# Decode products of a RetNet/HGRN2 step in plain float32 on the four column quarters of TensorE, with W_out loaded a second time

## The chip, the cores and the metric

The kernel runs on one core of a Trainium2 chip. The metric is the device time of one launch in microseconds (us). Three runs of the kernel before gave 1083.44, 1084.49 and 1085.34 us, so the median is 1084.49 us.

In what follows PE is TensorE's matmul, PEld its weight load, DVE is VectorE, ACT is ScalarE, POOL is GpSimd and SP is SyncE, which here only issues DMAs. A line such as L557 is a line of the kernel before; where the changed kernel is meant, the text says so.

## The reference

One layer is computed for a new prompt of 2048 tokens and for 8 sample tokens ("decode" below). Both share the weights. All data is float32.

```python
h = rmsnorm(x, norm_g)
rq, rk, rv, rg, hq, hf, hi, hgate = split(h @ w_in, 8)        # each 512 wide
# 4 retention heads of 128: rotary q and k, fixed decay per head
o_ret, s_ret_new = chunked_decay_recurrence(rq, rk, rv, log_gamma, s_ret)
# 4 HGRN2 heads of 128: silu(hq), gate f = lb + (1-lb) sigmoid(hf), k = 1-f
o_hg, s_hg_new = chunked_decay_recurrence(silu(hq), kin, hi, logf, s_hg)
# S_t = diag(f_t) S_{t-1} + k_t v_t^T ;  o_t = S_t^T q_t
o = concat(head_rmsnorm(o_ret) * silu(rg), head_rmsnorm(o_hg) * silu(hgate))
y = rmsnorm(x + o @ w_out, final_norm_g)
```

For the prompt the state starts at zero and the recurrence is done in chunks of 128 tokens. Each of the 8 decode tokens has a state of its own for each of the 8 heads (128x128), so that a head has one step `S = f*S + k v^T`, `o = S^T q` for each token. The new states of prompt and decode are outputs too.

## The kernel before

**Arithmetic.** Most matmuls run in fp32r with a split: an operand is written as a high and a low part (`hi_lo`, L106 on ACT and L107 on DVE), and a product is three matmuls (high·high, high·low, low·high; `three`, L292, and the projections, L557). The small score, state and transposition matmuls are plain float32.

**Stages, by the time in the profile.** From 7 to about 175 us stands the *values stage* (`pv`, L292): the 512+512 value columns of the projection for 16 token blocks. The first four blocks (pairs 0 and 1) are plain products, `pv0` while the weights still arrive, `pv1` after that; later pairs use a Strassen-like scheme of seven products, whose weight sums (`T1` to `T4`) are made by `wv_comb` on DVE, and whose token sums by `tok_ops`. From about 175 to 895 us stands the *recurrence stage*: 16 units of some 45 us, each with the projections of one head for one half of the prompt (L557) and, between them, the recurrence of the unit before. HGRN2 heads have score matmuls of 32 columns, which stand on the four column quarters of the array (`pah`, `plh`; L813, L832). From 895 to 957 us comes the *output stage* for the first token blocks (`py`, L1203), and from 957 to 1071 us six *out pairs* of 19 us (`po`, L292; pairs 2 to 7), again seven products of 12 matmuls each with operands that DVE makes out of `o_dram` (the steps `op_a`, `op_s12`, `op_s34`, `op_s23`, `op_s14`, `op_a22` for the pair that follows).

**Decode.** Three decode products are made with 40-column weights (8 columns of high part, 24 of zeros, 8 of low part) and 512 moving columns, 32 matmuls each:
- `pvd` (L400, `decode_values`): the values of the 8 tokens, after the plain products of block pair 1, 16 matmuls for each kind of head; `xs_hl` holds the split tokens.
- `pd` (L981, `d_mm`): `S^T q` of one head for all 8 tokens, against the split state `dsh`, `dsl` (made by `d_lo`: L969 on ACT, L973 on DVE). All 8x8 products of token and state are made and only the diagonal is used. Each head goes through `d_load`, `d_mul`, `d_add`, `d_lo` and two `d_mm`, at positions between units 8 and 15.
- `pyd` (L1029, `d_project`): the output projection, at 937 us; ahead of it `d_norm`, `d_sq`, `d_ms`, `d_rs` normalise and `d_tr` transposes, head by head (`pdt`, L1018).

**What sets the order.** PE's order is written out by hand, by the steps in program order and their positions (`place`, `merge`, `side_at`). On the other engines a scheduler orders the instructions by priority as their operands come free; SP, ACT's and POOL's queues issue their DMAs in that order, one after another. A tile pool of six 4 KB buffers, `rawp` (tag `raw`), holds the raw weights of the recurrence stage (`wr`), the decode states `dS`, the values `dv`, the splits `ds`, and in the out pairs `or` and `oS`; a new tile waits until the readers of the one that had its buffer are done.

Of the kernel before, what the change touches and what calls it, by code (L numbers as in the profile page):

```python
# [41 lines left out]
def step_kernel(ctx, tc, a, out):  # L42
# [15 lines left out]
    d_dram = dr.tile([8, 42240], F32, tag="d_dram", name="d_dram")  # L58
# [319 lines left out]
    xs_hl = vq.tile([P, KT, 40], F32R, tag="xs_hl", name="xs_hl")  # L378

    def decode_inputs():  # L380
        msd = sm.tile([NB, 2], F32, tag="msd", name="msd")
        for h in range(2):
# [6 lines left out]
        dve.tensor_tensor(xs, xs, g_in.unsqueeze(2).to_broadcast([P, KT, NB]), op=ALU.mult)  # L389
        act.activation(xs_hl[:, :, 0:8], xs, AF.Copy)  # L390
        act.activation(xs_hl[:, :, 8:32], zero.unsqueeze(1).to_broadcast([P, KT, 24]), AF.Copy)
        dve.tensor_tensor(
            xs_hl[:, :, 32:40], xs, xs_hl[:, :, 0:8].bitcast(F32), op=ALU.subtract
        )

    def decode_values(ty):
        ps = bank([40, GW], f"pvd{ty}")
        for k in range(KT):
            for n, w in enumerate(wv(f"B{k // 4 + 1}{ty + 1}", k % 4)):
                pe.matmul(ps, xs_hl[:, k], w, start=(k == 0 and n == 0), stop=(k == KT - 1 and n == 1))  # L400
        t1 = vq.tile([NB, GW], F32, tag="vo", name=f"vd1{ty}", bufs=2)
        act.activation(t1, ps[32:40, :], AF.Copy)
        t2 = vq.tile([NB, GW], F32, tag="vo", name=f"vd2{ty}", bufs=2)
        dve.tensor_tensor(t2, ps[0:NB, :], t1, op=ALU.add)
        dve.tensor_scalar(t2, t2, rsd[:, ty : ty + 1], None, op0=ALU.mult)
        sp.dma_start(vd_dram[ty], t2)
# [35 lines left out]
    wv_load(5)  # L442
    for k in (1, 5):
        x_split0(0, k)
        wv_split(k)
# [13 lines left out]
    sp.dma_start(pk, a["pack"])  # L459
# [20 lines left out]
    for ty in (1, 0):  # L480
# [10 lines left out]
        decode_values(ty)  # L491
# [437 lines left out]
    def d_split(src, name):  # L929
        pl, tag = (up, "dhl") if name == "dq_hl" else (rawp, "raw")  # L930
        t = pl.tile([P, 8, 40], F32R, tag=tag, name=name)
        act.activation(t[:, :, 0:8], src, AF.Copy)
        act.activation(t[:, :, 8:32], zero.unsqueeze(1).to_broadcast([P, 8, 24]), AF.Copy)
        dve.tensor_tensor(t[:, :, 32:40], src, t[:, :, 0:8].bitcast(F32), op=ALU.subtract)
        return t

# [18 lines left out]
    def d_add(hd):  # L955
# [6 lines left out]
        if hd == 0:  # L962
            dec["q"] = d_split(dq, "dq_hl")

    def d_lo(hd):
        ty, h = divmod(hd, NH)
        S, vb = dec["l", hd]
        sh, sl = (rawp.tile([P, NB, P], F32R, tag="raw", name=f"ds{t}{hd}") for t in "hl")
# [4 lines left out]
        dve.tensor_tensor(sl, S, sh.bitcast(F32), op=ALU.subtract)  # L973
        dec["s", hd] = (sh, sl)

    def d_mm(hd, part):
        for i in (part,):
            e = tp.tile([40, 512], F32, tag="tmp", name=f"de{hd}{i}")
            pt = ps_o.tile([40, 512], F32, tag="o", name=f"pd{hd}{i}")
            for n, t in enumerate(dec["s", hd]):  # L980
                pe.matmul(  # L981
                    pt, dec["q"][:, hd], t[:, i * 4 : i * 4 + 4], start=(n == 0), stop=(n == 1)
                )
            act.activation(e, pt, AF.Copy)
            act.dma_start(
                d_dram[hd, : 40 * D].rearrange("(r c) -> r c", c=D)[:, i * 512 : i * 512 + 512], e
            )

    def d_norm():
        dec["o2"] = []  # L990
        for n in range(2):
            x = rawp.tile([NB, 8, P], F32, tag="raw", name=f"do{n}")
            o0 = n * 32 * D
            pool.dma_start(
                x, d_dram[:, o0 : o0 + 8 * 1152].rearrange("u (b c) -> b u c", c=1152)[:, :, :P]
            )
            dec["o2"].append(x)

    def d_sq():
        o, sq = dec["o2"]  # L1000
        dve.tensor_tensor(o, o, sq, op=ALU.add)
        dve.tensor_tensor(sq, o, o, op=ALU.mult)

    def d_ms():
        ms = sm.tile([NB, 8], F32, tag="dms", name="dms")
        dve.tensor_reduce(ms, dec["o2"][1], axis=mybir.AxisListType.X, op=ALU.add)
# [3 lines left out]
    def d_rs():  # L1010
        o = dec["o2"][0]
        dve.tensor_tensor(o, o, dec["ms"].unsqueeze(2).to_broadcast([NB, 8, P]), op=ALU.mult)
        dec["o"] = o

    def d_tr():
        pt = ps_tr.tile([P, 8, NB], F32, tag="tr", name="pdt")
        for hd in range(8):
            pe.transpose(pt[:, hd], dec["o"][:, hd], ident[:NB, :NB])  # L1018
        dve.tensor_tensor(dq, pt, dg_, op=ALU.mult)
# [458 lines left out]
```

## Time and profile before

| | |
|---|---|
| median of three runs | 1084.49 us |
| the profiled execution, its time and its span | 1081.12 us, 1079.3 us |
| mean granted TensorE clock | 0.998 |
| PE busy | 1061.1 us, 98% |
| DVE busy | 742.4 us, 69% |
| ACT busy | 407.3 us, 38% |
| POOL busy | 125.8 us, 12% |
| moved by DMA | 146.76 MB, mean 136 GB/s |

The profiled execution is one launch; its time is 3.4 us below the median of the three others. Busy time of PE counts from a matmul's start to its modelled end, so that 98% busy does not say that matmuls start as fast as they can. A plain float32 matmul leaves two records in the trace, an fp32r matmul one.

### The profile page before, as it was taken

Reading aid. Unit: us, or ns where it says so; the run is one execution under the profiler, and the core shown is the slowest. Engines: PE = TensorE matmul, PEld = TensorE weight load, DVE = VectorE, ACT = ScalarE, POOL = GpSimd, SP = SyncE. Lnnn points to the kernel's source line nnn. Section 1 sums busy time; section 2 is a strip of 40 time slices with the busy share of each in tenths; the row PEclk is TensorE's granted clock in tenths of the full one; section 3 lists DMA queues with packets and bytes.
Section 4 is the critical chain, followed back from the end, with each engine's and each line's share of the span. In section 5 each row is a group of like instructions: output and inputs, shape, how many; then the busy total and the mean of one; then the engine's idle time right before and its main releaser. Section 6 shows DMA issues by size and latency. Waiting matters only on the chain.

```text
span 1079.3 us, 21758 instructions
## 1 busy us (share of the span) xinstructions
PE 1061.1 (98%) x9030; PEld 908.3 (84%) x9030; DVE 742.4 (69%) x1274; ACT 407.3 (38%) x872; POOL 125.8 (12%) x219
## 2 busy tenths in 40 slices
PE   9999999999999999999998999999999999999997
PEld 8778888989989999998987888888788788788885
DVE  7676987494675486478858646854954587359885
ACT  7763322242333323334433323433433254133432
POOL 1310000001101010010110101011010012321112
PEclk9999999999999999999999999999999999999999
DMA  8564448323421431352545126234432323686432
GB/s 299 198 201 160 137 123 287 125 101 99 156 81 56 141 99 41 114 174 71 179 118 155 44 96 154 54 106 129 129 100 68 105 81 124 229 308 201 160 136 98
DMA packets 103443, 146.76 MB, mean 136 GB/s; under 512 B 5872, under 2 KB 69488, under 8 KB 102576
## 3 DMA queue, kind: packets, MB, share of 16 engines
q1 hardware_dynamic: 82736, 105.94, 31.4%
q0 software_dynamic: 6992, 25.27, 6.2%
q10 hardware_dynamic: 13616, 14.16, 3.8%
q8 instruction: 71, 1.16, 0.4%
q14 instruction: 28, 0.23, 0.1%
HBM read 105.70 MB, written 39.65 MB: 135 GB/s over the span
## 4 chain that ended last, share of the span: by engine, by line
PE 89%; DVE 6%; DMA 3%; issue 1%; POOL 1%; ACT 1%; DVEq 0%; POOLq 0%; ACTq 0%; SPq 0%
PE pv L292 15%; PE pjg L557 14%; PE po L292 11%; PE pjfh L557 8%; PE pjqh L557 8%; PE pjkr L557 7%; PE pjqr L557 5%; PE py L1203 4%; DMA dv<-vd_dram 2%; PE pur L669 1%; PE puh L669 1%; PE par L728 1%; PE por L684 1%; PE poh L684 1%; PE poh L686 1%; PE por L686 1%
## 5 line engine op out<-in xcount | busy, mean ns | idle before, releaser
L557 PE MATMUL pjg<-xh,w_h 128*128 128x512 f32 (+2 forms) x320 | 115.6, 361 | 0.0
L557 PE MATMUL pjg<-xh,w_l 128*128 128x512 f32 (+2 forms) x320 | 111.3, 348 | 0.0
L557 PE MATMUL pjg<-xl,w_h 128*128 128x512 f32 (+2 forms) x320 | 110.9, 346 | 0.0
L106 ACT ACTIVATE w_h<-wr 128x1024 fp32r<-128x1024 f32 x48 | 50.9, 1061 | 87.1 <-PE pjg L557 32.6
L107 DVE TENSOR_TENSOR w_l<-wr,w_h 128x1024 fp32r<-128x1024 f32 x48 | 58.6, 1221 | 16.4 <-ACT w_h L106 7.8
L557 PEld LDWEIGHTS pjg<-xh,w_l 128*128 128x128 f32 x320 | 60.1, 188 | 7.9
L557 PEld LDWEIGHTS pjg<-xh,w_h 128*128 128x128 f32 x320 | 60.3, 188 | 6.7
L557 PEld LDWEIGHTS pjg<-xl,w_h 128*128 128x128 f32 x320 | 60.4, 189 | 6.3
L793 ACT ACTIVATE kepth<-kh 128x1024 f32<-128x1024 f32 x24 | 25.5, 1062 | 93.7 <-DVE kh L783 93.5
L557 PE MATMUL pjfh<-xh,w_h 128*128 128x512 f32 (+2 forms) x160 | 58.7, 367 | 0.0
L557 PE MATMUL pjqr<-xh,w_h 128*128 128x512 f32 (+2 forms) x160 | 58.0, 362 | 0.0
L557 PE MATMUL pjkr<-xh,w_h 128*128 128x512 f32 (+2 forms) x160 | 58.0, 362 | 0.0
L557 PE MATMUL pjqh<-xh,w_h 128*128 128x512 f32 (+2 forms) x160 | 57.3, 358 | 0.0
L557 PE MATMUL pjkr<-xh,w_l 128*128 128x512 f32 (+2 forms) x160 | 55.8, 348 | 0.1
L557 PE MATMUL pjfh<-xh,w_l 128*128 128x512 f32 (+2 forms) x160 | 55.7, 348 | 0.0
L557 PE MATMUL pjqh<-xh,w_l 128*128 128x512 f32 (+2 forms) x160 | 55.6, 348 | 0.0
L557 PE MATMUL pjqr<-xh,w_l 128*128 128x512 f32 (+2 forms) x160 | 55.6, 347 | 0.0
L557 PE MATMUL pjfh<-xl,w_h 128*128 128x512 f32 (+2 forms) x160 | 55.5, 347 | 0.0
L557 PE MATMUL pjkr<-xl,w_h 128*128 128x512 f32 (+2 forms) x160 | 55.5, 347 | 0.0
L557 PE MATMUL pjqr<-xl,w_h 128*128 128x512 f32 (+2 forms) x160 | 55.5, 347 | 0.0
L557 PE MATMUL pjqh<-xl,w_h 128*128 128x512 f32 (+2 forms) x160 | 55.5, 347 | 0.0
L591 ACT ACTIVATE sg<-pjg 128x512 f32<-128x512 f32 (+2 forms) x40 | 20.3, 507 | 62.3 <-PE pjg L557 62.2
(825 smaller groups left out, 2895.8 us busy)
## 6 DMA issues: line engine op xcount, KB each, us to landing
wr<-in_w_in SPq DMA_DIRECT2D x48, 512.0 KB, 3.4
xn<-in_x_prompt SPq DMA_DIRECT2D x32, 256.0 KB, 3.7
v_dram<-vo SPq DMA_DIRECT2D x32, 256.0 KB, 2.5
v<-v_dram SPq DMA_DIRECT2D x16, 512.0 KB, 3.7
or<-o_dram SPq DMA_DIRECT2D x16, 512.0 KB
xr<-in_x_t SPq DMA_DIRECT2D x12, 512.0 KB, 4.8
xr<-in_x_t SPq DMA_DIRECT2D x24, 256.0 KB, 4.2
xro<-in_x_prompt SPq DMA_DIRECT2D x12, 512.0 KB, 3.6
```

The costliest lines, as they stand in the source:

```text
L106: act.activation(h, src, AF.Copy)
L107: dve.tensor_tensor(l, src, h.bitcast(F32), op=ALU.subtract)
L292: pe.matmul(ps, xx, ww, start=(first and n == 0), stop=(last and n == 2))
L557: pe.matmul(ps, ww[:, kk], x[:, k, b0 : b0 + n], start=(k == 0 and i == 0), stop=(k == KT - 1 and i == 2),)
L591: act.activation(sg[:, :n], ps, AF.Sigmoid)
L669: pe.matmul(pu[:, j], ksb[g][:, j], vcol(4 * g + j), start=True, stop=True)
L684: pe.matmul(po[:, j], A[:, c], vcol(c), start=True, stop=src is None)
L686: pe.matmul(po[:, j], qcol(c), src, start=False, stop=True)
L728: pe.matmul(pa[:, j], k[:, cc], q[:, cc], start=True, stop=True)
L793: act.activation(ss[:, 512:], k[:, :HALF], AF.Copy)
L1203: pe.matmul(ps, o[:, kk], w[:, k % 4, i * 512 : (i + 1) * 512], start=(k == 0 and n == 0), stop=(k == KT - 1 and n == 2),)
```

## The change

All three decode products become plain float32 matmuls in groups of four. A group (`four`) multiplies the same 8 or 32 token columns with the four 256-column quarters of a 1024-column operand; quarter j writes to PSUM partitions 32j, and so stands on column quarter j of the array.

- *Values*: `decode_values(k)` reads the raw weight tile `wr[k]` and runs in two blocks of four groups between the plain products of block pair 0; `decode_values_out` evacuates where the second `pvd` block was. The split tile `xs_hl` and its three operations are gone. The packed constants `pk`, which hold the tokens, are loaded after the fourth pair of weight tiles instead of later. `wv_comb` writes into the raw weight tiles and so comes after the group that reads them.
- *Heads*: `d_mm` is one group on the state `dS` itself. `d_lo` with `dsh` and `dsl` is gone, with two of its four `raw` buffers; one evacuation of 128x256 takes the place of two of 40x512, and two DMAs of 4x128 write the diagonal.
- *Normalisation*: one load of 64x128 (`do`), a square with a sum on ACT, one scaling and one 64-row transposition, at the place in the output stage where `d_project` was.
- *Output projection*: W_out is loaded raw a second time (`wd0` to `wd7`, 512 KB each, on SP into `rawp`), and eight groups run in four blocks inside out pairs 4 to 6.
- *Order*: `queued` ties the steps that make the operands of the next out pair to the last DVE instruction ahead of them in program order.

```diff
-    def decode_values(ty):
-        ps = bank([40, GW], f"pvd{ty}")
-        for k in range(KT):
-            for n, w in enumerate(wv(f"B{k // 4 + 1}{ty + 1}", k % 4)):
-                pe.matmul(ps, xs_hl[:, k], w, start=(k == 0 and n == 0), stop=(k == KT - 1 and n == 1))
...
+    def four(ps, x, w, first, last):
+        for j in range(4):
+            pe.matmul(ps[32 * j : 32 * j + x.shape[1]], x, w[:, j * 256 : j * 256 + 256], start=first, stop=last)
+    def decode_values(k):
+        if not pvd:
+            pvd.append(bank([P, 256], "pvd"))
+        four(pvd[0], xs[:, k], wr[k].rearrange("p a b -> p (a b)"), k == 0, k == KT - 1)
...
     wv_load(5)
+    sp.dma_start(pk, a["pack"])
...
                     plain_k(0, pv0[c, ty], c, ty, k, k == 0, k == KT - 1)
+        if kk % 2:
+            for k in (kk - 1, kk, kk + 3, kk + 4):
+                decode_values(k)
...
-        act.activation(sh, S, AF.Copy)
...
-        dve.tensor_tensor(sl, S, sh.bitcast(F32), op=ALU.subtract)
...
+    def d_mm(hd):
+        S, vb = dec["l", hd]
+        e = tp.tile([P, 512], F32, tag="tmp", name=f"de{hd}")
+        pt = ps_o.tile([P, 256], F32, tag="o", name=f"pd{hd}")
+        four(pt, dec["q"][:, hd], S.rearrange("p b d -> p (b d)"), True, True)
+        act.activation(e[:, :256], pt, AF.Copy)
+        for i in range(2):
+            act.dma_start(d_dram[hd, i::2], e[i : i + 103 : 34, i * P : i * P + P])
...
+    def d_tr():
+        pt = ps_tr.tile([P, 8 * NB], F32, tag="tr", name="pdt")
+        pe.transpose(pt, dec["o"], ident[: 8 * NB, : 8 * NB])
...
+    def wd_load(k):
+        wd[k] = rawp.tile([P, D], F32, tag="raw", name=f"wd{k}")
+        before = next(i for i in reversed(nc.cur_bb.bb.instructions) if i.engine == sp.engine)
+        with tc.issue_after(before):
+            sp.dma_start(wd[k], a["w_out"][k * P : (k + 1) * P, :])
+    def wd_mm(k):
+        if k == 0:
+            wd["ps"] = ps_tr.tile([P, 256], F32, tag="tr", name="pyd")
+        four(wd["ps"], dq[:, k], wd[k], k == 0, k == KT - 1)
...
+    def queued(f):
+        before = next(i for i in reversed(nc.cur_bb.bb.instructions) if i.engine == dve.engine)
+        with tc.issue_after(before):
+            f()
...
             for f in after.get(step, ()):
-                f()
+                queued(f)
...
+    for n in range(4):
+        i, st_ = ((4, 0), (4, 4), (5, 1), (5, 4))[n]
+        wd_at[i] += [(st_, lambda n=n: wd_load(2 * n)), (st_, lambda n=n: wd_load(2 * n + 1))]
+        i, st_ = ((4, 3), (5, 0), (5, 4), (6, 1))[n]
+        wd_at[i] += [(st_, lambda n=n: wd_mm(2 * n)), (st_, lambda n=n: wd_mm(2 * n + 1))]
```

On PE, the first block of four groups in the values stage of the changed kernel stands in the middle of the plain products of pair 0. `wvr` are the raw weight tiles, `pk` the packed constants with the tokens, `wv` and `B` the split weights.

```order
L292 MATMUL pv_304<-B22l,xh_139 128x512
L292 MATMUL pv_304<-B22h,xl_140 128x512
L390 MATMUL pvd<-wvr_160,pk 8x256 x4
L390 MATMUL pvd<-wvr_180,pk 8x256 x4
L390 MATMUL pvd<-wvr_165,pk 8x256 x4
L390 MATMUL pvd<-wvr_182,pk 8x256 x4
L292 MATMUL pv_301<-wv_h,xh_139 128x512
```

Before, the same work stood behind pair 1, as 32 matmuls of 40x512; these four groups cover half of the contraction for all 1024 value columns.

On DVE, around the first decode head, the kernel before has the product with `dk`, the state's sum, and behind it the split `dsl`, ahead of the HGRN2 evacuations `qh` and `qth`.

```order
L950 TENSOR_TENSOR dv_6086<-dv_6086,dk 128x1024
L959 SCALAR_TENSOR_TENSOR dS_6085<-dS_6085,dv_6086 128x1024
L675 COPY str_5926<-pur_6026 128x128
L677 SCALAR_TENSOR_TENSOR str_5926<-str_5926,pur_6026 128x128 x2
L973 TENSOR_TENSOR dsl_6211<-dS_6085,dsh_6210 128x1024
L677 SCALAR_TENSOR_TENSOR str_5926<-str_5926,pur_6026 128x128
L642 TENSOR_TENSOR qh_5929<-pjqh_0_5994,qsh_6055 128x512
```

In the changed kernel the product with `dk` stands four instructions earlier, and nothing follows the state's sum.

```order
L947 TENSOR_TENSOR dv_6079<-dv_6079,dk 128x1024
L734 SCALAR_TENSOR_TENSOR A<-par_5975,pk 128x512
L638 TENSOR_SCALAR fh_5920<-fsh_5982,lb_126,lb 128x512
L641 TENSOR_SCALAR kh_5921<-fxh_5981,lb_126 128x512
L107 TENSOR_TENSOR xl_5929<-xr_6071,xh_5928 128x1024
L956 SCALAR_TENSOR_TENSOR dS_6078<-dS_6078,dv_6079 128x1024
L680 COPY str_5919<-pur_6019 128x128
L682 SCALAR_TENSOR_TENSOR str_5919<-str_5919,pur_6019 128x128 x3
L647 TENSOR_TENSOR qh_5922<-pjqh_0_5987,qsh_6048 128x512
```

On DVE in the out pairs, the kernel before makes the sums `oS_6` for pair 6 during pair 4 (`ou_4` and `po` around it are evacuations of pair 4, `op5S2l` the low part of an operand of pair 5).

```order
L1263 TENSOR_TENSOR oS_6_10746<-or_10707 128x512
L1269 TENSOR_TENSOR oS_6_10745<-or_10706,or_10707 128x512
L1340 TENSOR_TENSOR xro_10503<-po_10554,xro_10503 128x512
L1264 TENSOR_TENSOR oS_6_10745<-oS_6_10746,or_10706 128x512
L107 TENSOR_TENSOR op5S2l<-oS_5_10589,op5S2h 128x1024
L1270 TENSOR_TENSOR oS_6_10746<-or_10706,oS_6_10745 128x512
L1343 TENSOR_TENSOR ou_4_10587<-po_10574,os_4_10547 128x512
```

In the changed kernel they stand between the evacuations of pair 5.

```order
L1332 TENSOR_TENSOR ou_5_10643<-po_10630,os_5_10589 128x512
L1252 TENSOR_TENSOR oS_6_10646<-or_10593 128x512
L1341 TENSOR_TENSOR xro_10547<-xro_10547,ou_5_10643 128x512
L1334 TENSOR_TENSOR ou_5_10662<-po_10649,ou_5_10643 128x512
L1335 TENSOR_TENSOR xro_10545<-xro_10545,ou_5_10662 128x512
L1336 TENSOR_TENSOR xro_10547<-xro_10547,ou_5_10662 128x512
L1338 TENSOR_TENSOR xro_10545<-po_10668,xro_10545 128x512
L1253 TENSOR_TENSOR oS_6_10645<-oS_6_10646,or_10592 128x512
L1258 TENSOR_TENSOR oS_6_10645<-or_10592,or_10593 128x512
L1259 TENSOR_TENSOR oS_6_10646<-or_10592,oS_6_10645 128x512
```

So an operand that was ready a pair ahead is now made in the pair just before its use. On SP, in pairs 4 and 5 of the changed kernel, the raw weights `wd` stand in line with the loads `or` and `xro` of the next pairs.

```order
L1003 DMA wd_10423<-in_w_out 128x1024
L1003 DMA wd_10425<-in_w_out 128x1024
L1290 DMA xro_10374<-in_x_prompt 128x1024
L1290 DMA xro_10545<-in_x_prompt 128x1024
L1003 DMA wd_10520<-in_w_out 128x1024
L1003 DMA wd_10522<-in_w_out 128x1024
L1237 DMA or_10592<-o_dram 128x8x128
L1237 DMA or_10593<-o_dram 128x8x128
L1139 DMA yd<-in_x_sample 8x1024
L1290 DMA xro_10547<-in_x_prompt 128x1024
L1003 DMA wd_10626<-in_w_out 128x1024
L1003 DMA wd_10628<-in_w_out 128x1024
```

A load on SP that waits for its buffer holds up the ones behind it; `or_10592` and `or_10593`, the data of pair 6, are behind `wd_10520` and `wd_10522`, whose buffers come free when PE has used `wd_10423` and `wd_10425`.

More of the change, by code (lines that the diff above doesn't have):

```diff
@@ L388, in decode_inputs, with decode_values_out @@
         pool.tensor_scalar(rsd[:, 0:1], rsd[:, 1:2], KSCALE, None, op0=ALU.mult)
[L389 to L394, printed above, removed]
-    def decode_values(ty):
-        ps = bank([40, GW], f"pvd{ty}")
-        for k in range(KT):
-            for n, w in enumerate(wv(f"B{k // 4 + 1}{ty + 1}", k % 4)):
[L400 to L406, printed above, removed]
+    def four(ps, x, w, first, last):
+        for j in range(4):
+            pe.matmul(ps[32 * j : 32 * j + x.shape[1]], x, w[:, j * 256 : j * 256 + 256], start=first, stop=last)
+    pvd = []
+    def decode_values(k):
+        if not pvd:
+            pvd.append(bank([P, 256], "pvd"))
+        four(pvd[0], xs[:, k], wr[k].rearrange("p a b -> p (a b)"), k == 0, k == KT - 1)
+    def decode_values_out():
+        for ty in range(2):
+            t = vq.tile([NB, GW], F32, tag="vo", name=f"vd{ty}", bufs=2)
+            for n in range(2):
+                j = 2 * ty + n
+                act.activation(t[:, n * 256 : n * 256 + 256], pvd[0][32 * j : 32 * j + NB], AF.Copy)
+            dve.tensor_scalar(t, t, rsd[:, ty : ty + 1], None, op0=ALU.mult)
+            sp.dma_start(vd_dram[ty], t)
     dgd = vq.tile([NB, NB], F32, tag="dgd", name="dgd")
@@ L927, in step_kernel @@
     dec = {}
[L929 to L935, printed above, removed]
     def d_load(hd):
@@ L962, in d_add @@
         if hd == 0:
[L963 to L968, printed above, removed]
-        act.activation(sh, S, AF.Copy)
+            dec["q"] = up.tile([P, 8, 32], F32, tag="dqp", name="dqp")
+            dve.tensor_copy(dec["q"][:, :, 8:32], zero.unsqueeze(1).to_broadcast([P, 8, 24]))
+            dve.tensor_copy(dec["q"][:, :, 0:8], dq)
         act.dma_start(
@@ L972, in d_lo @@
         )
[L973 to L987, printed above, removed]
-    def d_norm():
[L990 to L1002, printed above, removed]
+    def d_mm(hd):
[6 more added lines that the diff above has]
+            act.dma_start(d_dram[hd, i::2], e[i : i + 103 : 34, i * P : i * P + P])
+    def d_norm():
+        x = sm.tile([8 * NB, P], F32, tag="old", name="do", bufs=1)
+        pool.dma_start(x, d_dram.rearrange("u b d -> (u b) d"))
+        dec["o"] = x
     def d_ms():
-        ms = sm.tile([NB, 8], F32, tag="dms", name="dms")
-        dve.tensor_reduce(ms, dec["o2"][1], axis=mybir.AxisListType.X, op=ALU.add)
+        x = dec["o"]
+        ms = sm.tile([8 * NB, 1], F32, tag="dms", name="dms")
+        jk = sm.tile([8 * NB, P], F32, tag="sf", name="dsq", bufs=1)
+        act.activation(jk, x, AF.Square, accum_out=ms)
         rsqrt_mean(ms, ms, P, EPS)
@@ L1022, in d_project @@
-    def d_project():
-        ps = [ps_o.tile([40, 512], F32, tag="o", name=f"pyd{i}") for i in range(2)]
-        t = rawp.tile([NB, 2, 512], F32, tag="raw", name="ydl")
-        for i in range(2):
-            m = 0
-            for k in range(KT):
-                for w in wo[k // 4]:
-                    pe.matmul(
-                        ps[i], dec["od"][:, k], w[:, k % 4, i * 512 : (i + 1) * 512],
-                        start=(m == 0), stop=(m == 2 * KT - 1),
-                    )
-                    m += 1
-            act.activation(t[:, i], ps[i][32:40], AF.Copy)
-        finish_y(ps, dec["y"], out["y_sample"], NB, "d", junk_op, add=[t[:, 0], t[:, 1]])
+        pt = ps_tr.tile([P, 8 * NB], F32, tag="tr", name="pdt")
@@ new lines, in wd_out @@
+    def wd_out():
+        y, ms = dec["y"], sm.tile([P, 2], F32, tag="yms", name="ymsd")[:NB]
+        for i in range(2):
+            cc = slice(i * GW, i * GW + GW)
+            t = op.tile([P, GW], F32, tag="t40", name=f"yd{i}")[:NB]
+            for n in range(2):
+                j = 2 * i + n
+                act.activation(t[:, n * 256 : n * 256 + 256], wd["ps"][32 * j : 32 * j + NB], AF.Copy)
+            dve.tensor_tensor(y[:NB, cc], y[:NB, cc], t, op=ALU.add)
+            act.activation(t, y[:NB, cc], AF.Square, accum_out=ms[:, i : i + 1])
+        pool.tensor_tensor(ms[:, 0:1], ms[:, 0:1], ms[:, 1:2], op=ALU.add)
+        rsqrt_mean(ms[:, 0:1], ms[:, 0:1], D, EPS)
+        dve.scalar_tensor_tensor(y[:NB], y[:NB], ms[:, 0:1], fg[:NB], op0=ALU.mult, op1=ALU.mult)
+        pool.dma_start(out["y_sample"], y[:NB])
@@ L1390, in step_kernel @@
             }
+        if i in wd_at:
+            for step, f in wd_at[i]:
+                after.setdefault(step, []).append(f)
         o_pair(i, after)
```

36 lines of the change are left out of this document (15 added, 21 removed).

## The prediction

> **What bounds the kernel now.** I read the page's busy shares and its chain that ended last first, then the chain in order of time, then the stages.
>
> ```profile
> span 1079.3 us, 21758 instructions
> PE 1061.1 (98%) x9030; PEld 908.3 (84%) x9030; DVE 742.4 (69%) x1274; ACT 407.3 (38%) x872; POOL 125.8 (12%) x219
> PE 89%; DVE 6%; DMA 3%; issue 1%; POOL 1%; ACT 1%; DVEq 0%; POOLq 0%; ACTq 0%; SPq 0%
> ```
>
> PE carries 89% of the chain. So a microsecond of matmul that goes is nearly a microsecond of time, and the remaining tenth, where DVE and DMA carry the chain, says where PE waits. The stretches of the span show the place:
>
> ```profile
> 560.00:600.00 40.00, 35.72 (x564) 28.64 (x563) 31.70 (x48) 15.11 (x22) 2.34 (x4) 1.00 0.47 129
> 1014.00:1033.00 19.00, 19.00 (x86) 15.73 (x85) 16.90 (x24) 7.38 (x14) 3.37 (x8) 1.00 0.42 149
> ```
>
> The columns are the length, then busy time of PE, PEld, DVE, ACT and POOL, the granted clock, DMA share and GB/s. In 560 to 600 us, where the first decode heads run, PE is idle for 4.3 us of 40. In an out pair (second row) PE has no gap, and DVE has 2.1 us left of 19.
>
> **What goes from PE.** The chain and the timeline show the three decode products:
>
> ```profile
> 40.34 3.71 PE pvd L400 x16
> 55.78 3.71 PE pvd L400 x16
> 920.95 0.59 PE pdt L1018 x8
> 937.70 7.42 PE pyd L1029 x32
> 564.97 0.40 PE L557 MATMUL pjg<-xh,w_l 128*128 128x512 f32 x1
> 565.21 0.40 PE L981 MATMUL pd<-dsh,dq_hl 128*40 128x512 f32 x1
> 565.44 0.39 PE L981 MATMUL pd<-dsl,dq_hl 128*40 128x512 f32 x1
> 565.67 0.40 PE L557 MATMUL pjg<-xh,w_h 128*128 128x512 f32 x1
> ```
>
> The matmuls start 0.23 us apart, though the duration says 0.40, because they overlap; the start distance is the price. They stand among the projections with no gap on either side. `pvd` takes 3.71 twice, `pyd` 7.42, and 32 `pd` at 0.233 take 7.5: 22.3 us. The eight transpositions take 0.59; one of 64 columns is left, so 0.5 goes. Removed: 22.8 us.
>
> **What a group of four costs.** No row shows a quarter-column matmul of 256 columns. The nearest are the small score matmuls on the same quarters, and the plain float32 matmuls of 128 columns:
>
> ```profile
> 905.57 0.89 PE pur L669 x8
> 848.88 0.39 PE L557 MATMUL pjqr<-xl,w_h 128*128 128x512 f32 x1
> 849.11 0.39 PE L557 MATMUL pjqr<-xh,w_l 128*128 128x512 f32 x1
> 849.43 0.73 PE L832 MATMUL pah<-qh,kh 128*32 128x32 f32 x62
> 849.98 0.19 PE L813 MATMUL pah<-qth,kh 128*32 128x16 f32 x1
> 850.64 0.50 PE L557 MATMUL pjqr<-xh,w_h 128*128 128x512 f32 x1
> 850.98 0.39 PE L557 MATMUL pjqr<-xl,w_h 128*128 128x512 f32 x1
> 851.21 0.40 PE L557 MATMUL pjqr<-xh,w_l 128*128 128x512 f32 x1
> ```
>
> `pur` has 128 columns: eight records, four matmuls, in 0.89 us, or 0.111 a record; 256 columns make 0.222 a record by proportion, 0.444 for the two records of a matmul. In `pah`, 32 matmuls of 32 columns (64 records; two of them are split off in the row) go from quarter to quarter, and the next line begins 0.55 to 0.57 us after the first: at most 0.071 for four. By `pur`'s proportion a record of 32 columns is 0.028, so one quarter alone needs 0.056 for its two records, and four one after another 0.222. So the four run side by side, with 0.015 of stagger. If the stagger adds, a group of 256 columns takes 0.46 us; if it scales, 0.57; if nothing overlapped, 1.78. I take 0.46, since starts apart by a fixed issue time fit a row of short matmuls best: 24 groups, 11.0 us (bounds 10.7 and 13.7, far end 42.6).
>
> Entering the quarter block takes 849.43−849.11 = 0.32 instead of 0.23; behind it the first projection is 0.34 ahead of the second instead of 0.23, and the last small matmul pays about 0.1 more. That is 0.3 us for a block, and the change makes 2 blocks for the values, 8 for the heads and 4 for the output: 14, or 4.2 us. The page "TensorEngine Tiling (Array Packing)" of the Trainium skill, section "Key Properties", says that changing the tiling mode drains TensorE, which speaks against many short blocks; the 0.3 us agree, and the 40-column matmuls, which show no such gap, paid none.
>
> PE's own work: −22.8 + 11.0 + 4.2 = −7.6 us.
>
> **What a rule would make of it.** In the rows the loads of the next quarter run under the matmuls:
>
> ```profile
> L832 PEld LDWEIGHTS pah<-qh,kh x512: 106/109/113, 212.8 to 850.0; 128*32 128x32 f32 x171
> ```
>
> Each load takes 0.109 us, and eight of them pass within 0.071, so they cannot be exposed there. The page "TensorE: Matmul & The Clock Gate" of the Trainium skill, "Part 3: Packing small matmuls — row/col tiling", says that a weight load overlaps running matmuls only when its row group differs, and all four quarters here use all 128 rows. By that rule, at this row's prices, a group would be eight times load and record, 8 x (0.109+0.222) = 2.6 us, and the time some 1127 us; the trace disagrees with it at 32 columns.
>
> **Where stalls go.** PE's waits in the three places where it is not fed:
>
> ```profile
> PE plh L813 <- ACT kepth L794: 1.9, 2, 1.2
> PE plh L858 <- ACT kepth L794: 1.0, 1, 1.0
> PE plh L813 <- DVE qth L786: 1.0, 1, 1.0
> PE plh L863 <- DVE qth L786: 1.1, 1, 1.1
> PE poth L699 <- DVE oth L701: 1.6, 1, 1.6
> 563.08 1.24 DVE w_l L107
> 564.33 6.30 DMA dv<-vd_dram
> 570.65 1.24 DVE dv L950
> 573.18 4.14 DMA out_new_ret_sample<-dS
> 577.39 5.91 DMA dv<-vd_dram
> L973 DVE TENSOR_TENSOR dsl<-dS,dsh x8: 1218/1223/1227, 541.7 to 790.8; 128x1024 fp32r<-128x1024 f32 x8
> ```
>
> The first three rows are from 560 to 600 us (3.9 us), the fourth from 770 to 785 us, where another of the second kind stands beside it (2.1 with it), the fifth from 895 us: 7.6 us. The chain names the cause of the first group. `dv` of the second head cannot be loaded before `w_l` frees a raw buffer, its 6.3 us landing leaves DVE waiting for it until 570.65, and the third head's `dv` waits again, for the store of the first state, to 577.39; from there DVE is behind, and `kepth` and `qth` arrive late. With `d_lo` gone each head needs two raw buffers instead of four and 1.22 us less DVE: both waits fall on buffers freed earlier, and eight `dsl`, 9.8 us, leave DVE. For the stall at 895 us, the chain shows POOL's queue:
>
> ```profile
> 890.91 0.65 POOL out_new_hgrn_prompt L883
> 892.52 1.90 POOL orsh L103
> ```
>
> The one normalisation DMA, now issued behind the unit's last work, and one pow on 64 rows leave that queue freer. Ends: all 7.6 us go, or none, and a later `dv` product merely stalls somewhere else (it now stands ahead of `A` and `kh` in DVE's order, so that a late `dv` would hold them). I take 5, nearer to the first end, since the buffer count that made the largest wait is what the change cuts.
>
> **What is uncovered.** Between the last plain products and `v_pair(2)` the second `pvd` block stood, and hid the chain of the token operands:
>
> ```profile
> 49.62 0.68 PE prs L236 x4
> 52.48 2.47 DVE L252 SCALAR_TENSOR_TENSOR xr<-xr,g_in,rst 128x256 f32<-128x256 f32 x6 [2.43 <-ACT rst L241]
> 56.33 0.69 DVE L107 TENSOR_TENSOR xl<-xr,xh 128x512 fp32r<-128x512 f32 x1 [1.38 <-ACT xh L106]
> 59.49 4.55 PE pv L292 x20
> ```
>
> From `prs` to the end of `xl` it is 57.02−49.62 = 7.4 us; to PE's first use it was 9.7, and without the block it is 6.0. Between 0 (ACT and DVE have less to do here, since the decode evacuations and `xs_hl` are gone) and 1.4 us: I take 0.8. In the first stage the load of `pk` shifts the later weight tiles, and `wv_comb` waits for PE's groups; the plain products of pair 1 stand between and cover the latter; 0.5 for both, ends 0 and 1.5.
>
> In the out pairs the operand sums move from a pair ahead to just before their use, on a DVE with 2.1 us to spare, and eight raw loads share the six buffers and SP with `or` and `xro`. A load of this size lands in:
>
> ```profile
> wor<-in_w_out SPq DMA_DIRECT2D x8, 512.0 KB, 3.7
> ```
>
> `or` of pair 6 stands behind two `wd`, which wait for PE's group: three in a line, 11 us, of which a pair's 19 us hide all unless DVE reaches `op_a` first. I take 1.0, ends 0 and 6 (2 for each of three pairs). New stalls: 2.3 us.
>
> **The sum.** −7.6 − 5 + 2.3 = −10.3 us. The profiled execution took 1081.1, which makes 1070.8; it lies 3.4 below the median, and on the median of the runs it is 1084.5 − 10.3 = 1074.2. Predicted: 1074 us.
>
> **The rivals.**
> - *The arithmetic only.* The stalls are moved, not removed: DVE's and SP's orders change everywhere, and those of 560 to 600 us hang on DMA landings of 6 us that the change does not shorten. Then −7.6 with up to 2.3 of new ones: 1077 to 1079. Against it: the chain names the buffers.
> - *A quarter's second record holds up the next quarter.* If matmuls start in order and a quarter's two records exclude each other, only every second record overlaps: four records' time, 0.89 us a group, 10.3 more: 1084.5, no change. Against it: for `pah` it would give 0.111 for four, and the row has 0.071. For it: 256 columns are not 32.
> - *No overlap at this length.* 1.78 us a group, 31.7 more: 1106. Only a limit on streaming four long operands at once would do it; no row bears on that.
> - *The out pairs become late* (the other side). DVE, tied to program order, waits for `or` behind `wd` behind PE, and the operands of the next pair come late in pairs 4 to 6. It decides when it costs over 12.5 us in three pairs, 4.2 each above the 2.1 that DVE has free, so with `or` over 6 us later than needed in each: 1087 to 1092. Against it: 11 us of loads in a 19 us pair.
>
> **How the numbers follow.** About 0.2%, 2.2 us, is what a measurement of this kernel can tell from no change. The forecast, with stalls between fully gone and half gone, 1067 to 1077, gets 0.60; the arithmetic alone 0.24; the in-order quarter 0.04; the out pairs 0.06; no overlap at all 0.03, its rule with it; the rest, 0.03, is a stall I have not seen, of either sign. All of the first two and hardly any of the others is faster: 0.85; same 0.06; slower 0.09. The low end takes in all stalls gone and none new, −15.2, 1069, and 3 us for the runs' level: 1066. The high end takes in the second case, half of the scaled price of a group and a few microseconds in the out pairs: 1082.
>
> **What would show it.** The 24 groups should start 0.45 to 0.57 us apart inside a block, with 0.3 us around it; 0.9 is the in-order rival, 1.8 the serial one. PE's waits in the decode heads should fall from 7.6 to 3 or less, and the second head's `dv` should be issued before 560 us. At `v_pair(2)` at most a wait of 1 or 2 us for `xl`. An out pair should stay at 19 us, with 1.2 more for each block of two groups. What would make this wrong most easily is a wait of PE for an operand in pairs 5 to 7.

## The result, and the profile after

The changed kernel takes 1088.32 us (median of 8 runs, 1086.09 to 1092.12) against 1083.65 us for the kernel before in the same comparison (8 runs, 1082.09 to 1085.34). The ratio is 1.0054, 95% interval 1.0039 to 1.0068: by the ratio 5.8 us slower (4.2 to 7.4; the two medians lie 4.7 apart), where 10 us faster were forecast. The profiled execution has a span of 1085.8 us.

The head of its page, busy time and share of each engine:

```profile
span 1085.8 us, 21915 instructions
PE 1059.2 (98%) x9119; PEld 901.4 (83%) x9119; DVE 728.1 (67%) x1258; ACT 392.1 (36%) x856; POOL 115.9 (11%) x218
```

DVE lost 14.3 us of work and ACT 15.2, and still the time rose. PE shows only 1.9 us less of busy time, but as said above, busy time is no measure of the pace; the starts are. The PE timeline around one block of each kind of decode product, with the matmul before and the two behind it (start, duration, and at the end the number of records):

```profile
564.30 0.40 PE L562 MATMUL pjg<-xh,w_l 128*128 128x512 f32 x1
564.63 0.64 PE L390 MATMUL pd<-dS,dqp 128*32 128x256 f32 x8
...
565.54 0.40 PE L562 MATMUL pjg<-xl,w_h 128*128 128x512 f32 x1
...
1006.38 0.39 PE L292 MATMUL po<-oT1h,op4S1l 128*128 128x512 f32 x1
1006.70 1.05 PE L390 MATMUL pyd<-wd,dq 128*8 128x256 f32 x16
...
1008.02 0.40 PE L292 MATMUL po<-wol,op4S1h 128*128 128x512 f32 x1
...
17.90 0.39 PE L292 MATMUL pv<-B22h,xl 128*128 128x512 f32 x1
18.22 1.91 PE L390 MATMUL pvd<-wvr,pk 128*8 128x256 f32 x32
...
20.40 0.40 PE L292 MATMUL pv<-wv_l,xh 128*128 128x512 f32 x1
```

From the start of the matmul ahead of a block to that of the second one behind it, less two usual distances of 0.23 us, a block of one group costs 0.78 us, of two 1.18, of four 2.04. That is a line: 0.42 us for each group and 0.36 for each block. The 8 blocks of the heads, 4 of the output and 2 of the values make 15.1 us; 15.2 were forecast. So on PE itself the change does what was forecast. What differs from the forecast is PE's waits. The view of PE's waits, before any selection by time (us in total, times, the longest):

```profile
PE plh L818 <- ACT kepth L799: 7.5, 4, 3.9
PE po L292 <- DMA wol<-t_draml: 1.2, 1, 1.2
PE pyd L390 <- DMA wd<-in_w_out: 1.2, 2, 0.9
PE plh L818 <- DVE qth L791: 1.2, 2, 0.9
...
PE po L292 <- DVE op3S1l L107: 1.0, 1, 1.0
PE po L292 <- DVE op3S2l L107: 1.0, 1, 1.0
PE pv L292 <- DVE xl L107: 0.8, 1, 0.8
```

The lines of the recurrence stand 5 higher than before (L818 is L813 of before). The wait of `poth` at 895 us (1.6 us before) is gone. The heads' waits, `plh`, have become larger instead of smaller (10.6 us by the whole view, 7.2 before), and the out pairs, which had none, now wait for `wol`, `wd` and the operands of pair 3. If every distance between two starts on PE above 0.42 us is summed, less 0.23 each, it is 10.0 us before and 23.3 after: 13.3 more (the starts 0.43 us apart, shown below, are counted in it). With −7.7 of PE's own work (22.8 less, 15.1 more) that is +5.6, most of the 6.5 us between the spans of the two profiled executions (1079.3 and 1085.8).

**The heads.** The tile view of `dv` in the changed kernel: its first line is the product on DVE, the second what DVE waited for ahead of it.

```profile
L947 DVE TENSOR_TENSOR dv<-dv,dk x8: 1224/1226/1250, 537.9 to 770.5; 128x1024 f32<-128x1024 f32 x8
...
  DMA dv<-vd_dram: 20.9, 8
```

The same line of the kernel before:

```profile
  DMA dv<-vd_dram: 10.0, 4
```

DVE waited at four heads; now it waits at all eight, in total twice as long. The loads themselves have become earlier: the third head's, from SP's timeline of before and of after,

```profile
577.39 0.37 SPq L942 DMA_DIRECT2D dv<-vd_dram  x1
```

```profile
567.26 1.05 SPq L939 DMA_DIRECT2D dv<-vd_dram  x1
```

is issued 10 us sooner. But its product now stands right behind that. DVE's timeline there, and below it PE's:

```profile
577.37 1.23 DVE L947 TENSOR_TENSOR dv<-dv,dk 128x1024 f32<-128x1024 f32 x1 [5.93 <-DMA dv<-vd_dram]
578.51 0.69 DVE L788 TENSOR_TENSOR kh<-kh,fh 128x512 f32<-128x512 f32 x1
579.11 0.69 DVE L791 TENSOR_TENSOR qth<-qth,fh 128x512 f32<-128x512 f32 x1
```

```profile
580.90 0.99 PE L818 MATMUL plh<-kepth 128*32 128x16 f32 x64 [3.91 <-ACT kepth L799]
...
585.65 0.63 PE L562 MATMUL pjqr<-xl,w_h 128*128 128x512 f32 x1
586.07 0.63 PE L562 MATMUL pjqr<-xh,w_l 128*128 128x512 f32 x1
...
588.52 0.40 PE L562 MATMUL pjqr<-xh,w_h 128*128 128x512 f32 x1
588.76 0.39 PE L562 MATMUL pjqr<-xl,w_h 128*128 128x512 f32 x1
```

DVE's queue holds the product with `dv` ahead of `kh` and `qth`, which need nothing of decode. `dv` has not landed, so `kh` and `qth` wait the 5.9 us behind it, the operands of `plh` come late, and PE stops for 3.9 us. Then something else shows: for nine matmuls PE's starts are 0.43 us apart instead of 0.23. The stretch 560 to 600 us has a granted clock of 0.91, where it was 1.00 before (the same columns as in the prediction):

```profile
560.00:600.00 40.00, 35.19 (x557) 27.92 (x556) 29.52 (x45) 12.21 (x19) 1.75 (x3) 0.91 0.50 137
```

So the wait is paid once as a wait and once more, some 1.9 us, as a slow clock.

**The out pairs.** ACT and DVE at the start of pair 2 in the changed kernel:

```profile
965.46 0.63 ACT L106 ACTIVATE op3A22h<-or 128x512 fp32r<-128x512 f32 x1 [21.10 <-DMA or<-o_dram]
...
968.31 0.58 ACT L1326 ACTIVATE os<-po 128x512 f32<-128x512 f32 x1
```

```profile
968.93 0.69 DVE L1327 TENSOR_TENSOR xro<-xro,os 128x512 f32<-128x512 f32 x1 [14.50 <-ACT os L1326]
```

ACT stands 21 us at `op3A22h`, for the load of pair 3's data; `os`, the evacuation of pair 2, is behind it; and DVE, tied to program order, is behind `os`. What DVE then makes for pair 3 comes about 1 us late at each of two places.

### The profile page after: what moved, and what is told of

Read it like the earlier page. It is cut to its first block, busy times and chain, and to the rows that moved or that the text cites. A ratio compares the mean times of both kernels' runs of the same rounds, so it can differ in the third digit from the quotient of the medians.

```text
span 1085.8 us, 21915 instructions
## 1 busy us (share of the span) xinstructions
PE 1059.2 (98%) x9119; PEld 901.4 (83%) x9119; DVE 728.1 (67%) x1258; ACT 392.1 (36%) x856; POOL 115.9 (11%) x218
```

## The experiments

All ratios are to the kernel before, run on the same chip in the same comparison, with a 95% interval.

### One part at a time

*The values alone* (`decode_values`, `decode_values_out`, the earlier load of `pk`; everything else as before):

> Only the decode values are changed (raw weights, groups of four, pk early); heads and output are as before. Theory (the groups cost what was summed, and the time was lost in new waits elsewhere): 7.4 us of 40-column matmuls go, two blocks of four groups at 2.04 us each come, and some 1.3 us are lost where v_pair(2) waits for xl, so 1.5 to 2.5 us faster than before. Rival (PE's gain is lost anyway, because every operand is made just in time and PE only waits for it sooner): within 0.7 us of before.

Measured: 1079.91 us, 0.998 (0.997 to 0.9989), −2.2 us. This part gives what the sum said of it: −7.4 of `pvd`, +4.3 for eight groups in two blocks and +1.3 uncovered make −1.8.

*The heads alone* (without `d_lo`; `d_mm` as one group on `dS`; the one-piece normalisation and transposition):

> Only the decode heads and their normalisation are changed (no split, one group of four a head, one load of 64x128, one transposition); values and the output projection are as before. Theory: PE's own work falls by 1.7 us and the wait at 895 us by 1.7 us, but DVE waits some 20 us for dv instead of 10 us and holds kh and qth back, so that the waits at plh and the halved clock behind them add 7 to 9 us: 3 to 6 us slower than before. Rival (the heads' stalls come from PE being ahead by the values' gain): no slower than before, 1 to 4 us faster.

Measured: 1086.56 us, 1.0041 (1.0029 to 1.0053), +4.5 us. PE's waits in it, first rows:

```profile
PE plh L813 <- ACT kepth L794: 6.6, 4, 3.0
PE plh L813 <- DVE qth L786: 2.5, 3, 1.1
```

Another 1.2 us in it is a wait of the transposition `pdt` for `do`, which the whole change does not have.

*The output projection alone* (W_out loaded raw, eight groups in pairs 4 to 6, `queued`; values and heads as before, the eight transpositions moved to where `d_project` was):

> Only the output projection is changed (W_out loaded raw again, eight groups in pairs 4 to 6, DVE order tied); values, heads and normalisation are as before. Theory: PE's own work falls by 2.7 us, and the out pairs lose 5 us to op3S, wol and wd: 1.5 to 3 us slower than before. Rival (the out pairs stalled only because PE came there early or late by what happened before): 1 to 3 us faster than before.

Measured: 1085.72 us, 1.0032 (1.0021 to 1.0043), +3.6 us, a little above what was expected. The three parts make −2.2 + 4.5 + 3.6 = +5.9, the whole. So two of three parts cost time, each by itself, and they can be looked into separately.

### The heads: what holds DVE

If the late `dv` is what holds `kh`, then a kernel without that load should have no such waits. In `d_load`, the load is left out, and `d_mul` multiplies `dk` by ones:

```diff
-        sp.dma_start(vb, vd_dram[ty, :, h * P : (h + 1) * P].partition_broadcast(P))
...
-            dve.tensor_tensor(vb, vb, kd, op=ALU.mult)
+            dve.tensor_tensor(vb, ones.unsqueeze(1).to_broadcast([P, NB, P]), kd, op=ALU.mult)
```

> The kernel with only the heads changed, with the load of dv left out: the product with dk takes ones instead, so the decode states and outputs are not the reference's; the buffers stay. Theory (DVE waits for a dv that lands late): DVE's 20 us of waits for dv go, the waits at plh fall to below 3 us and the clock stays full; 1080 us or less. Rival (the reordering of DVE's work itself, not the landing, delays kh and qth): the waits at plh stay above 5 us, some 1086 us.

Measured: 1075.31 us, 0.9942 (0.993 to 0.9954), 11.3 us less than the heads alone (1086.56). It also takes 4 MB off the DMAs, so it does not tell the order from the load; and 3.8 us of waits for `plh` stay in it. The next one keeps every instruction and moves only the order: `d_mul` and `d_add` (with the store of the new state that `d_add` issues) are tied behind the last DVE instruction ahead of them in program order, so that the scheduler can't draw them forward.

```diff
+    def tied(f, *args):
+        before = next(i for i in reversed(nc.cur_bb.bb.instructions) if i.engine == dve.engine)
+        with tc.issue_after(before):
+            f(*args)
...
-        steps = [d_load, lambda hd: d_mul(hd, 0), lambda hd: d_mul(hd, 1), d_add, d_mm]
+        steps = [d_load, lambda hd: tied(d_mul, hd, 0), lambda hd: tied(d_mul, hd, 1), lambda hd: tied(d_add, hd), d_mm]
```

> The kernel with only the heads changed, and in it d_mul and d_add tied to program order on DVE, so that a dv that has not landed no longer stands ahead of kh and qth; loads and buffers are as there. Theory (DVE's order: kh and qth wait behind the product with dv): the 7 us of waits at plh between 576 and 782 us with the halved clock behind them shrink to 1 to 3 us, and the time to 1079 to 1082 us, 1 to 3 us faster than before. Rival (the raw buffers are the limit, and hold up wr when dv is used later): new waits for w_h at the projections, no faster than the kernel with only the heads changed, 4 us slower than before.

Measured: 1071.59 us, 0.9904 (0.9891 to 0.9917), −10.5 us, far better than expected. The tile view of `dv` and the stretch 560 to 600 us of this kernel:

```profile
L955 DVE TENSOR_TENSOR dv<-dv,dk x8: 1215/1216/1221, 557.3 to 825.9; 128x1024 f32<-128x1024 f32 x8
```

```profile
560.00:600.00 40.00, 40.00 (x598) 32.29 (x597) 30.60 (x54) 13.87 (x21) 2.71 (x4) 1.00 0.40 112
```

The first product stands at 557 us (538 in the whole change, 538.5 in the heads alone), DVE does not wait for `dv` once, PE is busy for all of the 40 us and the clock is 1.00. The largest wait for `plh` left in the whole kernel is 0.4 us.

Does the gain belong to the new heads, or to the tie? The kernel before with the same tie for its `d_mul`, `d_add` and `d_lo`, and nothing else:

```diff
-        steps = [d_load, lambda hd: d_mul(hd, 0), lambda hd: d_mul(hd, 1), d_add, d_lo,
+        steps = [d_load, lambda hd: tied(d_mul, hd, 0), lambda hd: tied(d_mul, hd, 1), lambda hd: tied(d_add, hd),
+                 lambda hd: tied(d_lo, hd),
```

> The kernel before with d_mul, d_add and d_lo tied to program order on DVE and nothing else altered. Theory (the order on DVE is what made the waits, before too): the 7.6 us of waits at plh and poth and 1 to 2 us of half clock largely go, 1075 to 1078 us. Rival (only the new heads, with two buffers less each, can afford the later product): the four raw buffers of a head are held longer, wr comes late, and the time stays within 2 us of before or rises.

Measured: 1076.27 us, 0.995 (0.9932 to 0.9969): −6.5 us between the medians, −7.4 to −3.4 by the interval. So by the medians some six tenths of the 10.5 are the tie's, and the new heads give some 4 to 5 on top of it (1.4 of PE's work and 0.5 of transpositions were forecast). The six runs of this kernel spread from 1073.98 to 1080.70 us, so that the split is rough: the two profiled executions, with spans of 1072.1 and 1069.3 us, are only 2.8 apart, which those 1.9 and 0.9 us less in distances over 0.42 us make up. By DVE's order alone, with its buffers as they were, the kernel before is rid of nearly all its stalls in the decode heads: of 7.2 us of waits for `plh`, 0.5 are left.

### The out pairs: what makes them late

First the tie alone. The kernel before, with `queued` around the steps that make the operands of the next pair:

```diff
             for f in after.get(step, ()):
-                f()
+                queued(f)
```

> The kernel before with nothing but the tie of DVE's order in the out pairs. Theory A (the tie: operands of pair 3 wait in line behind the evacuations of pair 2): PE waits 1 us each for op3S2 and op3S1, 1.5 to 3 us slower than before. Theory B (PE came to the out pairs 7 us earlier while the data of pair 3 still lands at 964 us): no waits, within 1 us of before.

Measured: 1083.05 us, 1.0009 (1.0 to 1.0017), and no wait in the out pairs. Then the changed kernel without the tie (the reverse edit):

> The changed kernel without the tie of DVE's order in the out pairs (the scheduler may again make operands a pair ahead); all else as changed. Theory: of the 5 us lost in the out pairs the 2.2 us at op3S go and perhaps the 1.2 us at wol and 1.2 us at wd: 2 to 4 us faster than the changed kernel, some 1085 us. Rival (buffers and SP's line, not the tie, make the operands late): within 1 us of the changed kernel.

Measured: 1091.31 us, 1.0082 (1.0067 to 1.0097): not better, but 3 us worse than with it. PE's first wait and the row of DVE that causes it:

```profile
PE po L292 <- DVE op2S2l L107: 8.0, 1, 8.0
```

```profile
964.76 0.69 DVE L1252 TENSOR_TENSOR oS<-or 128x512 f32<-128x512 f32 x1 [22.15 <-DMA or<-o_dram]
965.37 1.22 DVE L107 TENSOR_TENSOR op2S2l<-oS,op2S2h 128x1024 fp32r<-128x1024 f32 x1
```

The scheduler put a sum of pair 3, whose data is not there yet, ahead of an operand of pair 2: the same mechanism as with `dv`, one 8 us wait in place of several small ones. The tie, which the prediction's rival of late out pairs suspected, is here a remedy, if an incomplete one.

Next, ACT: since `os` stands behind `op3A22h`, ACT was tied to program order as well, in the output part alone and in the whole change with tied heads (which is described below).

```diff
-        before = next(i for i in reversed(nc.cur_bb.bb.instructions) if i.engine == dve.engine)
-        with tc.issue_after(before):
+        last = [next(i for i in reversed(nc.cur_bb.bb.instructions) if i.engine == e.engine) for e in (dve, act)]
+        with tc.issue_after(last[0]), tc.issue_after(last[1]):
```

> Only the output projection changed, as in the third run, with ACT tied too. Theory: 2 to 4 us faster than with DVE alone tied, so 0 to 2 us slower or faster than before. Rival: 3 to 4 us slower than before, as with DVE alone tied.

> As the kernel with tied heads, and in the out pairs the steps are tied to the last ACT instruction too, so that ACT's op3A11h and op3A22h, which wait for the data of pair 3, no longer stand ahead of the copy os of pair 2. Theory (the DVE tie made the evacuations of pair 2 wait for ACT's line, which waited 21 us for the load of pair 3): the 2 us at op3S2 and op3S1 go, with what they delay; 2 to 4 us faster than with DVE alone tied, 1068 to 1070 us. Rival (the landing of the loads at 964 us sets the operands whatever the order): the waits stay, within 1 us of that kernel.

Measured: 1086.86 us, 1.0039 (1.0026 to 1.0053) for the first, against 1085.72 without; 1072.44, 0.991 (0.9896 to 0.9923) for the second, against 1071.86. No gain. In the first the waits for `op3S1l` and `op3S2h` went (2.3 us), those for `wol` (1.5 us) and `op3S2l` (1.3) stayed, that for `wd` grew from 0.4 to 1.1, and in pair 7 a new one came (`op7S2l`, 1.0, and 1.9 in the second). So ACT's order decides which operand is late, but putting it right does not bring the time back.

Last, PE's time of arrival. Without `d_project`, PE reaches the out pairs about 7 us sooner, and the stretch ahead of them is full of transfers. The windows 936 to 960 us, of before and then of the output part alone (the last three columns are clock, DMA share and GB/s):

```profile
936.00:960.00 24.00, 24.00 (x107) 17.37 (x106) 9.13 (x13) 5.80 (x12) 3.31 (x6) 1.00 1.07 401
```

```profile
936.00:960.00 24.00, 24.00 (x112) 19.69 (x111) 6.97 (x10) 3.35 (x6) 2.30 (x5) 1.00 1.06 399
```

In both, all 16 DMA engines are busy at 400 GB/s for 24 us, with `T` tiles, which take the place of the recurrence stage's tiles and are issued from 933.68 us on before and from 933.82 in the output part alone. So the landing of pair 3's data did not move either, though its loads were issued 6 and 8 us sooner (942.62 and 943.05 us, 948.87 and 951.20 before): `op3A22h` starts at 963.87 us before and at 964.25 in the output part alone. PE, 7 us sooner, now waits for what it met ready before:

```profile
PE po L292 <- ACT op3S2h L106: 1.3, 1, 1.3
PE po L292 <- DMA wol<-t_draml: 1.2, 1, 1.2
PE po L292 <- DVE op3S2l L107: 1.1, 1, 1.1
PE po L292 <- DVE op3S1l L107: 1.0, 1, 1.0
```

To test this reading, matmuls of about the length of `d_project` were put back in its place, with no use of their result: 32 of 40x512 on W_out's split tiles in the first, 33 float32 matmuls of 128x128 on ones in the other two.

```diff
+    def cover():
+        ps = ps_tr.tile([P, P], F32, tag="tr", name="pcv")
+        for i in range(33):
+            pe.matmul(ps, ones, ones, start=True, stop=True)
...
-        (0.36, lambda: t_load("T3", (0, 1))), (0.42, d_tr),
+        (0.36, lambda: t_load("T3", (0, 1))), (0.42, d_tr), (0.42, cover),
```

> Only the output projection changed, and 32 matmuls of 40x512 on W_out, whose results are used by nothing, stand where d_project was, so that PE comes to the out pairs as late as before. Theory (PE's early arrival uncovered the loads): no waits for op3S or wol, 7.4 us of matmuls more than without cover and some 4 us of waits less: 1088 to 1089 us. Rival (the waits come from the tie alone): the waits stay, 1093 us.

> Only the output projection changed, and 33 plain float32 matmuls of 128x128 on the tile of ones, read by nothing, stand where d_project was: 7.4 us of PE that touch no weight, buffer or queue of the output stage. Theory (PE's early arrival uncovered the loads of the T tiles and of pair 3): the waits for op3S and wol go, only those for wd stay, and the time is before + 4.8 for the groups + 1: 1087 to 1088 us. Rival (tie and raw loads make the waits whenever PE comes): the 5 us of waits stay, 1091 to 1093 us.

> The output part alone, with 33 float32 matmuls of 128 columns on ones (66 records at 0.111 = 7.3 us) put ahead of the transposition of the decode tokens, where the PSUM bank is free: in the run before, the same cover stood behind the transposition and waited 5.1 us for the evacuation dq to free the bank, so that PE came some 15 us later, not 7. The output part alone gave 1085.7, with waits of 4.6 us for wol, op3S2h, op3S2l and op3S1l. Theory 'PE now comes to the out pairs 7 us sooner than their operands are ready': 1085.7 + 7.3 - 4 to 5 = 1088 to 1089, with at most 1 us of these four waits left. Rival 'the waits come from the raw loads and the shifted orders and stay whenever PE comes': 1085.7 + 7.3 = 1093, with the waits there.

In the third, the cover stands ahead of `d_tr`. Measured: 1091.55 us, 1.009 (1.0073 to 1.0107); 1094.88, 1.0117 (1.0103 to 1.0132); 1091.45, 1.0087 (1.0073 to 1.0101). In the second, PE waited for `dq` to free the cover's bank, and then ran the cover on a slow clock; the third had neither:

```profile
942.61 10.09 PE L1388 MATMUL pcv<-ones 128*128 128x128 f32 x66 [5.12 <-DVE dq L1024]
```

```profile
936.77 7.53 PE L1388 MATMUL pcv<-ones 128*128 128x128 f32 x66
```

The second came 14 us later to the out pairs than the output part alone, and there the four waits are gone altogether; what is left in its out pairs is `wd`, 1.3 us. The first and the third came 7 us later, at the time of the kernel before. Of the 4.6 us the first kept 2.7 (`op3S1l` 1.5, `wol` 1.2); in the third these are left:

```profile
PE po L292 <- DVE op3S1l L107: 1.5, 1, 1.5
PE pyd L930 <- DMA wd<-in_w_out: 1.4, 1, 1.4
PE po L292 <- DMA wol<-t_draml: 0.6, 1, 0.6
PE po L292 <- DVE op3S2l L107: 0.5, 1, 0.5
```

So a part of the waits, 2 of 4.6 us, goes when PE arrives later, and the rest does not, while the wait for `wd` grew by 1.0: the time came out nearer to the rival's 1093 than to 1088 or 1089. That rest is not settled, because the covers moved the other engines' orders too. In all three ACT had `op3A22h`, which stood 17 us until pair 3's data landed, ahead of `op2S2h` and of a square `yj` for the token blocks before; POOL waited for `yj` until 963 us, and only behind that issued `woh`, and at 969 to 970 `wol`, where the output part alone issued them at 949.93 and 962.93. No run had PE late and the orders unmoved.

### What is left when the order is mended

The whole change with tied heads:

> The changed kernel with d_mul and d_add tied to program order, nothing else altered. Theory (the heads' and the output's losses are separate): the values and tied heads together took 13.5 us off, the output change alone put 3.6 on, so 10 us faster than before, some 1072 us. Rival (arriving still earlier, PE meets the burst of loads ahead of the out pairs sooner and loses more there): 1075 us or more.

Measured: 1071.86 us, 0.9903 (0.9889 to 0.9916). The order of some 20 DVE instructions (8 products with `dk`, 4 with the HGRN2 gate, 8 sums) moves the change from +5.8 to −10 us. And the values and heads with the tie, the output projection as before:

> Values changed, heads changed and tied as above, output projection as before: the two parts that should gain, together. Theory: -2.2 us of the values and what the tied heads give, 1077 to 1079 us. Rival (the parts compete for the same slack): no better than the values alone, 1080 us.

Measured: 1068.53 us, 0.9875 (0.9862 to 0.9888), 13.5 us faster than the kernel before and 3.3 faster than the whole change with the tie. It is the best version here; by the sum above, distances over 0.42 us cost it 4.5 us of waits, and the raw W_out with its 4 blocks is a loss in either company (+3.6 and +3.3).

## Why the prediction was wrong

*What is removed from PE, and what a group and a block cost:* right in the main. 0.46 us for a group and 0.3 for a block were forecast, 0.42 and 0.36 measured. That the sums agree to 0.1 us is luck: 24 groups came out 1.0 cheaper and 14 blocks 0.8 dearer. Of the two choices for the stagger the fixed one (0.46) was much nearer than the scaled one (0.57); the measured group leaves no room for a stagger. The rival of the in-order quarter (0.89) and that without overlap (1.78) are excluded. The page "TensorE: Matmul & The Clock Gate" of the Trainium skill, "Part 3: Packing small matmuls — row/col tiling", would have made a group 2.6 us by its rule that a load overlaps only with another row group; the trace disagrees also at 256 columns, with 0.42.

*Where stalls go:* this term failed, in sign and size. The prediction took −5 us, because fewer raw buffers would let `dv` be loaded earlier. They did: the second head's `dv` is issued at 556.54 us, before the 560 that the prediction named, and the third's 10 us sooner. But the scheduler put the product with `dv` forward in DVE's queue by as much, so that it still waits, at every head, and now ahead of work that PE needs. The prediction even named the effect ("a late `dv` would hold them") but counted it at most as a gain that does not come, not as a loss; the order showed the first head's product ahead of `A`, and what stood behind it at the third, `kh` and `qth`, was not looked up. By the runs, the heads cost +4.5 where −1.4 of PE's work, −0.5 of transpositions and −5 were forecast: 11.4 of the 16 us between forecast and result. That it is the order is shown by the tie (−10.5 with all instructions kept) and that it was so before by the tie on the kernel before (−6.5): the chain had shown `dv` twice, and "the load is late" was read from it where "the product stands too early" was as good a reading. The prediction also put all the stalls between 560 and 600 us behind the third head's `dv`, issued at 577.39. In the kernel before the `kh` and `qth` of the first stall ran ahead of that, at 576.59 and 577.19, behind the second head's product, sum and split; only later ones stood behind the third head's product (583.39), which waited 0.9 us.

*What is uncovered in the values stage:* right within what can be told. 1.3 us were taken; that part alone gave −2.2 where its sum makes −1.8. In the whole change the wait for `xl` is 0.8 us.

*The out pairs:* 1.0 us was taken, with 6 as the far end, and this place was named as the likeliest to make the forecast wrong. The part costs +3.6 where −2.5 of PE's work (with 1.0 of new waits −1.5) was forecast: 5.1 us too low. The mechanism was not the one of the rival ("waits for `or` behind `wd` behind PE" in pairs 4 to 6): the waits are in pairs 2 and 3, ahead of any `wd`, for pair 3's operands and `wol`, and the tie of DVE is not their cause. What was missed is that `pyd` was also cover: 7 us of PE's work under a DMA burst of 24 us that ends when it did before, so that what PE saves there can come back as waits. How much of the waits is this, and how much the moved orders, stays open, as said.

*The clock:* not in the prediction at all. It added about 1.9 us behind the 3.9 us wait, and 1.4 behind a second one at 776 us.

With 11.4 and 5.1 too low and 0.4 gained in the values, the difference between −10.3 and +5.8 is accounted for.

## What to carry to other kernels

When an edit frees a buffer, ask not only what can be loaded earlier but what the scheduler will then queue earlier, and whom it stands in front of: the price of a late load is the time that the instructions behind its consumer wait, and here tying some 20 instructions of the decode heads to program order was worth 16 us to the changed kernel and 6.5 to the kernel before. Work that is removed from the bottleneck engine can be worth less than its length when what ends next is a transfer whose start does not move. In this kernel a wait of the matmul engine of more than about 2 us cost another 1 to 2 us of slow clock.

## What the runs showed of the hardware

**A wait costs clock.** After long waits PE started its 512-column matmuls 0.43 us apart instead of 0.23, for some 4 us at most. The shortest wait with that effect was in the kernel before with the tie of the out pairs, 2.16 us from start to start:

```profile
577.61 0.39 PE L557 MATMUL pjqr<-xh,w_l 128*128 128x512 f32 x1
579.77 0.74 PE L813 MATMUL plh<-kepth 128*32 128x16 f32 x64 [1.77 <-ACT kepth L794]
...
582.66 0.63 PE L557 MATMUL pjqr<-xh,w_l 128*128 128x512 f32 x1
583.09 0.63 PE L557 MATMUL pjqr<-xh,w_h 128*128 128x512 f32 x1
```

In all the profiled executions here, start distances of 2.16 to 8.4 us were followed by it, single ones of up to 1.97 us (at `poth`, 895 us) never. The length of one wait does not decide alone: two shorter ones with only small `plh` matmuls between them were followed by it in two runs (1.45 and 1.26 us in the values alone, 0.99 and 1.18 in the second cover), but 1.42 and 1.26 in the kernel before were not. The two covers above show it on equal work: 66 records took 10.09 us behind a 5.1 us wait, 7.53 without one. The page "TensorE: Matmul & The Clock Gate" of the Trainium skill, "Part 1: The HAM clock gate", says that the clock falls to half after an idle window of about 3.4 us and returns after about as long a busy one. The half rate and the length agree with the rows; that it takes 3.4 us of idleness does not, since 2.16 from start to start sufficed here.

**Four column quarters run side by side at full length.** A group of four float32 matmuls of 128x256 passes in 0.42 us, no more than one such matmul would by the proportion of the 128-column rows (0.44). Its eight weight loads of 0.085 to 0.11 us each would make 0.7 us or more in a line, so they are hidden.
